# A hybrid S5 and retention layer on one core: an early read of kst in each S5 chunk, later S5 parameters and scaled q, and squares of x behind the next weight cast

## The chip, the cores and the metric

The kernel runs on one core of one Trainium2 chip. The metric is the device time in microseconds (us) of one execution of the whole program; less is better. Three runs of the kernel before gave 1424.38, 1423.64 and 1424.18, a median of 1424.18.

## The reference

One layer of a decoder for 256 prompt positions and 8 samples of 8 positions, 320 rows of x with 2048 columns in all, in float32. In short:

```
h = rms_norm(x, norm_mix)
u, q, k, v, g = split(h @ w_in)             # 1024 columns each
y = s5_mixer(u)                             # 64 groups of 16 channels, 64 complex states each
y = gelu(y + d*u); y = y * sigmoid(y @ w_glu + b_glu)
o = retention(rotary(q), rotary(k), v)      # 8 heads of 128, decay per head, chunks of 128
o = silu(g) * group_norm(o)
x = x + concat(y, o) @ w_out
x = x + (silu(gate) * up) @ w_ffn_out       # gate, up = split(rms_norm(x, norm_ffn) @ w_ffn_in)
return rms_norm(x, norm_final), the S5 states, the retention states
```

## The kernel before, in words

x lies transposed: 128 channels on the partitions, 320 rows as columns, 16 such pieces. Every weight matrix is cut in blocks of 128 columns by 8 pieces of 128 rows (512 KB). SyncE (SP) loads a block into raw, ScalarE (ACT) casts it to hi in a shorter float format (line 133), VectorE (DVE) takes lo = raw - hi (line 135). raw, hi and lo have three buffers each, so the load of a block waits for DVE's lo of the block three before it, and the cast to hi waits until TensorE (PE) has read the hi of three before. A product is three matmuls per piece: hi with xhi, hi with xlo, lo with xhi (lines 145 to 147), 24 matmuls for a block, all summed in PSUM.

**First stage** (lines 954 to 980). Four outputs (two blocks of u, q and k of head 0) are accumulated together while x arrives, piece by piece and then in pairs. For each pair ACT and DVE make xhi and xlo (split_x, lines 269 to 276), ACT casts the weights (line 967), DVE makes lo (line 968), and ACT squares x in place for the norm (square_x, line 280). Their place in ACT's queue comes from priorities. DVE's s5_params and s5_params2 work out powers of the S5 eigenvalues from then on; POOL makes exponentials for them.

**Projections and heads** (lines 1014 to 1035). PE's order is written out by hand: projections run one after the other, and a clock in the program (clk.now, advanced with each product) decides after which matmul a piece of other work is put in. For a head: rot turns q and k by the rotary angles on DVE (lines 725 to 733), do_q multiplies the sample part of q by a decay into qg (lines 893 to 896), head_k transposes k into pst, copies it to kd on ACT and makes the scores pss, head_v transposes v and makes the outputs po, the group norm and the new state.

**S5 chunks** (s5_chunk, from line 577). Eight chunks of eight groups. A chunk first writes u to DRAM (via) and reads it back in another layout into kst: eight DMAs on SP's queue (line 590), which kst's two buffers share between chunks. Some time later (DL["b1"]) PE transposes four blocks bl into pt (line 624), and ACT copies pt into bst. Later again (DL["b2"]) PE makes the outputs py of the chunk before (s5_outputs, which reads toe and kst of that chunk), and then pb from bst and kst (line 639). ACT copies a part of pb into toe, six DMAs on SP spread it in toe (line 654), and DVE scans over the positions. toe and pb have one buffer each.

SP issues all loads of weights, kst, toe and the rest in one queue, one after the other; its order, and those of ACT and DVE, come from a scheduler by priorities and dependencies. Two words of the language: issue_after(i) keeps instructions behind i in their engine's order, and high_priority lifts them in it.

Of the kernel before, what the change touches and what calls it, by code (L numbers as in the profile page):

```python
# [12 lines left out]
F32 = mybir.dt.float32  # L13
F32R = mybir.dt.float32r
I32 = mybir.dt.int32
AF = mybir.ActivationFunctionType
ALU = mybir.AluOpType
ADD, SUB, MUL = ALU.add, ALU.subtract, ALU.mult
PSUM = bass.MemoryType.PSUM

P = 128
D = 2048
KT = D // P
NP, NB, NS = 256, 8, 8
# [8 lines left out]
CH = 4  # L33
NCP = NP // CH
NC = N // CH
# [11 lines left out]
def hybrid_kernel(ctx, tc, xT, w_in, w_in4, w_out, w_glu, w_fi, w_fo, w_fot, gfr, vecs, s5p, bc, x0,  # L47
# [3 lines left out]
    pe, act, dve, pool, sp = nc.tensor, nc.scalar, nc.vector, nc.gpsimd, nc.sync  # L51

    cst = ctx.enter_context(tc.tile_pool(name="cst", bufs=1))
# [3 lines left out]
    def f(t):  # L57
        return t.bitcast(F32)


    ident = cst.tile([P, P], F32, name="ident")
    make_identity(nc, ident)
    ones = cst.tile([P, P], F32, name="ones")
    pool.memset(ones, 1.0)
    mhalf = cst.tile([P, 4], F32, name="mhalf")
    pool.memset(mhalf, -0.5)
    vec = cst.tile([P, vecs.shape[1]], F32, name="vec")
# [35 lines left out]
    def mm(cost, *a, **k):  # L103
        pe.matmul(*a, **k)
        clk.now += cost
# [73 lines left out]
    def tt(out, a, b, op):  # L179
        dve.tensor_tensor(out, a, b, op)  # L180
        return out
# [15 lines left out]
    EVAC = 1500  # L197
# [39 lines left out]
    ps_b = s5stack.enter_context(tc.tile_pool(name="ps_b", bufs=1, space=PSUM))  # L237
# [3 lines left out]
    def misc(name):  # L241
        used["misc"] = clk.now
        return ps_m.tile([P, 512], F32, name=name, tag="misc", bufs=2)
# [25 lines left out]
    def split_x(k0, k1):  # L269
        for k in range(k0, k1):  # L270
            xr = xrs[k // 4][:, k % 4]
            if k == 0:
                tt(xhi[:, k], xr, v("g_mix", k).to_broadcast([P, N]), MUL)
            else:
                act.mul(xhi[:, k], xr, v("g_mix", k))
            dve.scalar_tensor_tensor(xlo[:, k], xr, v("g_mix", k), f(xhi[:, k]), MUL, SUB)

    def square_x(k0, k1):
        xr = xrs[k0 // 4][:, k0 % 4:(k1 - 1) % 4 + 1]
        act.activation(xr, xr, AF.Square)  # L280
        if k1 == 8:
            tt(u32[:, 0:4], u32[:, 0:4], u32[:, 4:8], ADD)
        elif k1 == 12:
            tt(u32[:, 0:4], u32[:, 0:4], retp[:, 0:4], ADD)
        elif k1 > 12:
            a = u32[:, 0:2]
            tt(a, a, u32[:, 2:4] if k1 == 14 else retp[:, 6:8], ADD)
            if k1 == 14:
                tt(a, a, retp[:, 4:6], ADD)
            else:  # L290
                tt(a[:, 0], a[:, 0], a[:, 1], ADD)
        return u32[:, 0]
# [126 lines left out]
    def s5_params2(used):  # L419
        newscr(1)  # L420
        scr[1] = used
        tt(lp[:, 0, 0], rr, ec[:, 0], MUL)
        tt(lp[:, 1, 0], rr, es[:, 0], MUL)
        den = tt(T(sh), prm[:, 0], prm[:, 0], MUL)
        d2 = tt(T(sh), prm[:, 1], prm[:, 1], MUL)
        tt(den, den, d2, ADD)
        rden = T(sh)
        dve.reciprocal(rden, den)
        rot_t["rden"] = rden
# [147 lines left out]
    def s5_chunk(c):  # L577
# [42 lines left out]
            tbl = s5_table(c)  # L620
        bst = s5.tile([P, 4, P], F32, name="bst", tag="bst", bufs=1)
        pt = misc("pt")
        for i in range(4):
            tr(pt[:, P * i:P * i + P], bl[:, i // 2, i % 2].rearrange("p u e h -> p (u e h)"))
        with tc.high_priority(offset=EVAC):
# [3 lines left out]
        if c:  # L629
            while clk.now - used["misc"] < MISC:  # L630
                yield 0.4
            pending.pop()()
        pb = ps_b.tile([P, 2, 512], F32, name="pb", tag="pb", bufs=1)
        for i in range(4):
            for u in range(2):

# [20 lines left out]
        if c < 7:  # L657
            pending.append(lambda: s5_outputs(c, kst, cl, xp))
            return
        yield DL["scan"]  # L660
        while clk.now - used["misc"] < MISC:
            yield 0.4
        s5_outputs(c, kst, cl, xp)
# [54 lines left out]
    rot_t = {}  # L718

    def rot(ps, name):  # L720
        assert rot_t["ready"]
        with tc.high_priority(offset=EVAC):
            return rot_(ps, name)

    def rot_(ps, name):
        sw = mp.tile([P, N], F32, name="sw", tag="sw", bufs=1)
        act.copy(sw[0:64], ps[64:128])
        rot_t["keys"] = act.copy(sw[64:128], ps[0:64])
        a = mp.tile([P, N], F32, name=name, tag=name, bufs=1)
        tt(a, ps, csr[:, 0], MUL)  # L730
        tt(sw, sw, csr[:, 1], MUL)
        tt(a, a, sw, ADD)
        return a

    def head_k(h, q_, qg, k_, R):
# [25 lines left out]
    def head_v(h, v_, qg, rt, R):  # L761
# [5 lines left out]
        with tc.high_priority(offset=EVAC):  # L767
            for i in range(3):
                act.mul(vT[:, i], pst2[:, P * i:P * i + P], rtok[:, i:i + 1])
        act.copy(vsp[64 * (h % 2):64 * (h % 2) + 64], vT[64:128, 2])  # L770
        last = act.copy(vs[:, h], vT[64:128, 2])
        if h == 0:
            rot_t["values"] = last
# [24 lines left out]
        with tc.high_priority(offset=GN):  # L798
            for i in range(nt):
                dve.bn_stats(st[:, i], po[:, i])  # L800
                dve.bn_aggr(mv[:, :, i], st[:, i])

        m_, t_, y_, w_ = mv[:, 0], mv[:, 1], y[:, 0], y[:, 1]
        pool.tensor_scalar(m_, m_, -1.0, None, MUL)
# [6 lines left out]
        pool.tensor_tensor(w_, m_, y_, MUL)  # L811
        if h == 0:
            rot_t["first"]()
        on = mp.tile([P, 3, P], F32, name="on", tag="on", bufs=1)

        def normed():
# [59 lines left out]
    def do_q(h, ps=None):  # L876
        ps = proj(8 + 4 * h) if ps is None else ps
        R = HS[h]
        rt = mp.tile([P, NB, P], F32, name="rt", tag="rt", bufs=2)
        R["rt"] = rt  # L880
        for i in range(2 if h == 1 else min(h, 1)):
            i = i if h == 1 else h
            with tc.issue_after(last_raw[0].ins) if h == 1 else nullcontext():
                sp.dma_start(HS[i]["rt"], r0[i])
        mk = mp.tile([P, NP + P], F32, name="mk", tag="mk", bufs=2)
        n = NP + P if h % 2 else NP
        with nullcontext() if h else tc.issue_after(last_raw[0].ins):
            sp.dma_start(mk[:, 0:n], masks[h, :, 0:n])
        R["mk"] = mk
        q_ = rot(ps, "q_")  # L890
        pool.tensor_copy(qsp[:, 64 * (h % 2):64 * (h % 2) + 64], q_[:, NP:N])
        qg = qgs[h % 2]
        for u in range(2):
            tt(qg[:, u].rearrange("p (b w) -> p b w", w=40)[:, :, 0:NS],
               q_[:, NP + 32 * u:NP + 32 * u + 32].rearrange("p (b t) -> p b t", t=NS),
               gqt[:, h].unsqueeze(1).to_broadcast([P, 4, NS]), MUL)
        R.update(q_=q_, qg=qg)
        run_due()

    def do_k(h, ps=None):  # L900
        ps = proj(9 + 4 * h) if ps is None else ps
        R = HS[h]
        k_ = rot(ps, "k_")
        pool.tensor_tensor(kvf[:, h], k_[:, NP:N].rearrange("p (b t) -> p b t", t=NS),
                           kdt[:, h].unsqueeze(1).to_broadcast([P, NB, NS]), MUL)
        pool.tensor_copy(ksp[:, 64 * (h % 2):64 * (h % 2) + 64], k_[:, NP:N])
        spawn(head_k(h, R["q_"], R["qg"], k_, R))
        run_due()
# [45 lines left out]
    for k1 in (1, *range(2, KT + 1, 2)):  # L954
        with tc.high_priority(offset=100000), tc.manual_schedule(engines={mybir.EngineType.SP}):
            if k0 % 2 == 0:
                raw, hi, lo = (wp.tile([P, 8, P], d, name=n, tag=n, bufs=3).rearrange("p (k o) m -> p k o m", o=4)
                               for n, d in (("raw", F32), ("hi", F32R), ("lo", F32R)))
            q = slice(k0 % 2, (k1 - 1) % 2 + 1)
            sp.dma_start(xrs[k0 // 4][:, k0 % 4:(k1 - 1) % 4 + 1], xT[:, k0:k1])  # L960
            (sp if k0 else act).dma_start(raw[:, q], w_in4[:, k0:k1])
            if not k0:
                sp.dma_start(vec, vecs)
            if k1 == 4:
                sp.dma_start(prm, s5p)
            split_x(k0, k1)
            act.copy(hi[:, q], raw[:, q])
            los.append(dve.tensor_tensor(lo[:, q], raw[:, q], f(hi[:, q]), SUB))
        if k1 == 4:
            exps = s5_exps()  # L970
        if k1 % 2 == 0:
            with tc.high_priority(offset=50000):
                accq = square_x(k1 - 2, k1)
        for k in range(k0, k1):
            for w_, x_ in ((hi, xhi), (hi, xlo), (lo, xhi)):
                for i, ps in enumerate(accs):
                    pe.matmul(ps, w_[:, k % 2, i], x_[:, k], start=k == 0 and w_ is hi and x_ is xhi,
                              stop=k == KT - 1 and w_ is lo)
            clk.now += 1.6
        k0 = k1  # L980
# [8 lines left out]
    def finish_norm():  # L989
        next(rg)  # L990
        act.copy(rtok, ytok[0])
        yield 4.5
        rps = next(rg)
        with tc.high_priority(offset=EVAC):
            act.copy(rbc, rps)
            tt(csr[:, 0], csr[:, 0], rbc, MUL)
            turned = dve.tensor_tensor(csr[:, 1], csr[:, 1], rbc, MUL)
            tt(u32[:, 0], ps0, rbc, MUL)
            tt(u32[:, 1], ps1, rbc, MUL)
        rot_t["ready"] = True  # L1000

        with tc.issue_after(turned.ins):
            s5_params2(exps[1])

    spawn(finish_norm(), DL["nm"])

# [538 lines left out]
```

## Time and profile before

| what | value |
|---|---|
| median of three runs | 1424.18 us |
| the profiled execution | 1424.95 us |
| its span | 1423.2 us |
| PE busy | 1415.5 us, 99% |
| DVE, ACT, POOL busy | 957.9, 606.5, 122.8 us |
| DMA, mean over the span | 188 GB/s |

The profile is one execution taken by the hardware profiler. PE is TensorE, DVE VectorE, ACT ScalarE, POOL GpSimd, SPq SyncE's queue of DMA issues. A row of a timeline gives start, duration, engine, line, operation, output<-inputs, shape, count, and in brackets the idle time of the engine before it with what ended it. A row of the list of waits gives who waited for whom, then us in total, times, longest us. A row of a table by stretches gives the stretch, its length, the busy time (and instructions) of PE, PE's weight loads, DVE, ACT and POOL, then the granted clock of PE as a share of full speed, the DMA share and GB/s. Names such as kst stand for every buffer of that name.

### The profile page before, as it was taken

The numbers are of one execution on the slowest core, as the hardware profiler recorded it, in microseconds if no ns is written. First come the engines' busy times: TensorE is split into PE (matmuls) and PEld (weight loads), VectorE is DVE, ScalarE is ACT, GpSimd is POOL, SyncE is SP. The second block draws the span as 40 slices with busy tenths as digits, with TensorE's granted clock in tenths as the row PEclk, the third lists the DMA queues.
The fourth block names the chain that finished last, engine by engine and source line by source line (L and its number), as shares of the span: only waits on it lengthen the run. The fifth ranks groups of instructions, "written<-read, shape, count | busy, mean of one in ns | idle before, by whom it ended". The sixth has DMA issues, their size and how long they took to land.

```text
span 1423.2 us, 26196 instructions
## 1 busy us (share of the span) xinstructions
PE 1415.5 (99%) x10376; PEld 1406.6 (99%) x10376; DVE 957.9 (67%) x1842; ACT 606.5 (43%) x973; POOL 122.8 (9%) x194
## 2 busy tenths in 40 slices
PE   9999999999999999999999999999999999999998
PEld 8999999999999999999999999999999999999998
DVE  7979878787557747777777545767644677655453
ACT  6654555555455443333333333333333333334553
POOL 7720111110000000100001000000000000000002
PEclk9999999999999999999999999999999999999999
DMA  8554555555644466675666446666545765445542
GB/s 278 170 187 158 163 174 157 171 163 157 218 156 151 164 209 228 221 253 201 245 206 231 136 148 238 233 216 235 170 146 175 255 233 190 159 157 184 154 143 75
DMA packets 102316, 267.07 MB, mean 188 GB/s; under 512 B 27377, under 2 KB 42033, under 8 KB 102193
## 3 DMA queue, kind: packets, MB, share of 16 engines
q1 hardware_dynamic: 101904, 265.01, 55.9%
q8 instruction: 81, 1.33, 0.4%
q10 hardware_dynamic: 288, 0.39, 0.1%
q14 instruction: 43, 0.34, 0.1%
HBM read 254.44 MB, written 10.52 MB: 186 GB/s over the span
## 4 chain that ended last, share of the span: by engine, by line
PE 96%; DVE 2%; DMA 1%; ACT 1%; issue 1%; POOL 0%; SPq 0%; POOLq 0%; DVEq 0%; ACTq 0%
PE ps_fg L147 7%; PE ps_fu L147 7%; PE ps_fu L146 7%; PE ps_fg L146 7%; PE ps_fg L145 7%; PE ps_fu L145 7%; PE ps_fo L147 7%; PE ps_fo L145 7%; PE ps_fo L146 7%; PE ps_p L145 6%; PE ps_p L147 6%; PE ps_p L146 6%; PE ps_o L145 2%; PE ps_o L146 2%; PE ps_o L147 2%; PE ps_t L1342 1%
## 5 line engine op out<-in xcount | busy, mean ns | idle before, releaser
L133 ACT CAST hi<-raw 128x1024 fp32r<-128x1024 f32 (+1 forms) x410 | 397.8, 971 | 684.2 <-PE ps_fg L146 182.3
L135 DVE TENSOR_TENSOR lo<-raw,hi 128x1024 fp32r<-128x1024 f32 (+1 forms) x410 | 462.8, 1129 | 304.2 <-ACT hi L133 301.3
L147 PE MATMUL ps_fg<-hhi,lo 128*128 128x320 f32 x704 | 218.0, 310 | 0.0
L147 PE MATMUL ps_fu<-hhi,lo 128*128 128x320 f32 x704 | 217.9, 310 | 0.0
L145 PE MATMUL ps_fg<-hhi,hi 128*128 128x320 f32 x704 | 217.9, 310 | 0.0
L146 PE MATMUL ps_fu<-hlo,hi 128*128 128x320 f32 x704 | 217.9, 310 | 0.0
L145 PE MATMUL ps_fu<-hhi,hi 128*128 128x320 f32 x704 | 217.9, 310 | 0.0
L146 PE MATMUL ps_fg<-hlo,hi 128*128 128x320 f32 x704 | 217.9, 310 | 0.0
L145 PE MATMUL ps_fo<-ahl,hi 128*128 128x320 f32 x671 | 208.0, 310 | 0.0
L147 PE MATMUL ps_fo<-ahl,lo 128*128 128x320 f32 x671 | 207.7, 310 | 0.0
L146 PE MATMUL ps_fo<-ahl,hi 128*128 128x320 f32 x671 | 207.7, 310 | 0.0
L145 PE MATMUL ps_p<-xhi,hi 128*128 128x320 f32 x560 | 177.3, 317 | 0.0
L147 PE MATMUL ps_p<-xhi,lo 128*128 128x320 f32 x560 | 173.3, 309 | 0.0
L146 PE MATMUL ps_p<-xlo,hi 128*128 128x320 f32 x560 | 173.1, 309 | 0.0
L147 PEld LDWEIGHTS ps_fg<-hhi,lo 128*128 128x128 f32 x704 | 132.2, 188 | 0.0
L146 PEld LDWEIGHTS ps_fu<-hlo,hi 128*128 128x128 f32 x704 | 132.2, 188 | 0.0
L146 PEld LDWEIGHTS ps_fg<-hlo,hi 128*128 128x128 f32 x704 | 132.2, 188 | 0.0
L145 PEld LDWEIGHTS ps_fg<-hhi,hi 128*128 128x128 f32 x704 | 132.2, 188 | 0.0
L147 PEld LDWEIGHTS ps_fu<-hhi,lo 128*128 128x128 f32 x704 | 132.1, 188 | 0.0
L145 PEld LDWEIGHTS ps_fu<-hhi,hi 128*128 128x128 f32 x704 | 132.1, 188 | 0.0
L146 PEld LDWEIGHTS ps_fo<-ahl,hi 128*128 128x128 f32 x671 | 126.0, 188 | 0.0
L147 PEld LDWEIGHTS ps_fo<-ahl,lo 128*128 128x128 f32 x671 | 126.0, 188 | 0.0
(476 smaller groups left out, 2117.8 us busy)
## 6 DMA issues: line engine op xcount, KB each, us to landing
raw<-w_fi SPq DMA_DIRECT2D x176, 512.0 KB, 4.2
raw<-w_in SPq DMA_DIRECT2D x79, 512.0 KB, 4.1
raw<-w_fo SPq DMA_DIRECT2D x61, 512.0 KB, 3.5
raw<-w_out SPq DMA_DIRECT2D x32, 512.0 KB, 3.7
hi<-vd SPq DMA_DIRECT2D x32, 512.0 KB, 5.4
lo<-vd SPq DMA_DIRECT2D x32, 512.0 KB, 5.2
raw<-w_fo SPq DMA_DIRECT2D x61, 192.0 KB, 2.4
rt<-r SPq DMA_DIRECT2D x8, 512.0 KB, 5.2
```

Source lines behind the costliest of these rows:

```text
L133: cast = act.copy(hi[:, :m], raw[:, :m])
L135: last_lo[0] = dve.tensor_tensor(lo[:, :m], raw[:, :m], f(hi[:, :m]), SUB)
L145: pe.matmul(ps, hi, xhi[:, k], start=k == 0, stop=False)
L146: pe.matmul(ps, hi, xlo[:, k], start=False, stop=False)
L147: pe.matmul(ps, lo, xhi[:, k], start=False, stop=k == nk - 1)
L1342: pe.matmul(ps[0:m, 0:TC], a3[:, x_, k, s:s + m], w_[:, k], start=k == 0 and x_ == 0 and w_ is whi, stop=k == FCT - 1 and w_ is wlo)
```

## The change

- **Early read of kst.** In s5_chunk, for chunks 1 to 7, pb is allocated ahead of the transposes, and a matmul of 3 columns by 1 reads toe and kst of the chunk and writes three unused values of pb, ahead of the transposes pt. Its result is not used.
- **First stage.** The squares of pairs (0,1) and (2,3) and those after them are issued behind the next pair's cast, the split of x and the cast behind an earlier square; the cast of the second pair is split in two halves, and so is its lo. ones is set by DVE, not POOL.
- **Head 0.** s5_params2 is issued behind the rotation of k and no longer behind the scaling of csr. The scaled q of head 0 (qg) is issued behind head 0's group statistics.
- **Small.** The copy to vsp gets a higher priority for odd heads; the last chunk's outputs wait 1.2 longer on the program's clock.

```diff
@@ s5_chunk
         pt = misc("pt")
+        pb = ps_b.tile([P, 2, 512], F32, name="pb", tag="pb", bufs=1)
+        if c:
+            mm(0.06, pb[0:CH - 1, 1, 4 * NC:4 * NC + 1], toe[:, 0, 0:CH - 1, 0], kst[:, 0, 0:1], start=True, stop=True)
         for i in range(4):
...
-        pb = ps_b.tile([P, 2, 512], F32, name="pb", tag="pb", bufs=1)
...
-        yield DL["scan"]
+        yield DL["scan"] + 1.2
@@ head_v
-        act.copy(vsp[64 * (h % 2):64 * (h % 2) + 64], vT[64:128, 2])
+        with tc.high_priority(offset=EVAC if h % 2 else 0):
+            act.copy(vsp[64 * (h % 2):64 * (h % 2) + 64], vT[64:128, 2])
...
         if h == 0:
             rot_t["first"]()
+            with tc.issue_after(aggr.ins):
+                R["scaled_q"]()
@@ do_k
         k_ = rot(ps, "k_")
+        if not h:
+            with tc.issue_after(rot_t["turned"].ins):
+                s5_params2(exps[1])
@@ the first stage
-            split_x(k0, k1)
-            act.copy(hi[:, q], raw[:, q])
-            los.append(dve.tensor_tensor(lo[:, q], raw[:, q], f(hi[:, q]), SUB))
+            with tc.issue_after(sq[-1].ins) if len(sq) > 1 and k1 < 10 else nullcontext():
+                split_x(k0, k1)
+                for q in ([slice(i, i + 1) for i in range(2)] if k1 == 4 else [q]):
+                    cast = act.copy(hi[:, q], raw[:, q])
+                    los.append(dve.tensor_tensor(lo[:, q], raw[:, q], f(hi[:, q]), SUB))
...
-        if k1 % 2 == 0:
-            with tc.high_priority(offset=50000):
-                accq = square_x(k1 - 2, k1)
+        for k2 in {1: (), 2: (), 4: (2,), 6: (4,), 8: (6, 8)}.get(k1, (k1,)):
+            with tc.high_priority(offset=50000), tc.issue_after(cast.ins):
+                accq = square_x(k2 - 2, k2)
```

What stands in the engines' orders, before and now. First ACT's queue at the start of the first stage: hi is the weight cast, xhi the scaled x, u<-u the square. Before:

```order
L967 CAST hi<-raw 128x512
L275 ACTIVATE xhi<-u_119,vec 128x320
L967 CAST hi<-raw 128x512
L280 ACTIVATE u_119<-u_119 128x640
L275 ACTIVATE xhi<-u_119,vec 128x320 x2
L967 CAST hi<-raw 128x1024
L280 ACTIVATE u_119<-u_119 128x640
```

Now:

```order
L984 CAST hi<-raw 128x512
L275 ACTIVATE xhi<-u_119,vec 128x320
L984 CAST hi<-raw 128x512
L275 ACTIVATE xhi<-u_119,vec 128x320 x2
L984 CAST hi<-raw 128x512 x2
L282 ACTIVATE u_119<-u_119 128x640
```

The first square has moved behind the second pair's cast, and this cast is two.

Next PE's queue at chunk 2, inside a projection (ps_p); bl is what is transposed into pt. Before:

```order
L145 MATMUL ps_p_2065<-xhi_101,hi_2054 128x320
L146 MATMUL ps_p_2065<-xlo_102,hi_2054 128x320
L147 MATMUL ps_p_2065<-xhi_101,lo_2055 128x320
L109 MATMUL pt_2079<-ident_64,bl_1888 128x128 x4
L145 MATMUL ps_p_2065<-xhi_101,hi_2054 128x320
```

Now:

```order
L145 MATMUL ps_p_2068<-xhi_101,hi_2057 128x320
L146 MATMUL ps_p_2068<-xlo_102,hi_2057 128x320
L147 MATMUL ps_p_2068<-xhi_101,lo_2058 128x320
L104 MATMUL pb_2083<-kst_1873,toe_144 3x1
L109 MATMUL pt_2082<-ident_64,bl_1891 128x128 x4
L145 MATMUL ps_p_2068<-xhi_101,hi_2057 128x320
```

The new matmul stands at the place of the transposes, and reads chunk 2's kst, kst_1873. In chunks 1 to 5 it does so between the same matmuls as the transposes before; in chunks 6 and 7 both stand three projection matmuls earlier.

Last SP's queue for the same chunk, now, with the semaphores that SP waits for: the last six of the eight pieces of kst_1873, and the weight loads (raw) between them.

```order
L592 DMA kst_1873<-via_1871 16x4x80 [waits DMAHW7_49]
L592 DMA kst_1873<-via_1871 16x4x80 [waits DMAHW0_49]
L592 DMA kst_1873<-via_1871 16x4x80 [waits DMAHW1_49]
L132 DMA raw_2314<-w_in 128x1024 [waits DMAHW2_49,DVE_49]
L592 DMA kst_1873<-via_1871 16x4x80 [waits DMAHW3_49]
L592 DMA kst_1873<-via_1871 16x4x80 [waits DMAHW4_49]
L132 DMA raw_2320<-w_in 128x1024 [waits DMAHW5_49,DVE_49]
L592 DMA kst_1873<-via_1871 16x4x80 [waits DMAHW6_49]
```

Here nothing has moved: the queue before reads the same with line 590 in place of 592. In chunks 5 and 6 one piece of kst is left behind the last such weight load, where there were two and three.

On DVE at head 0 the scaled q stood between the rotations of q and k, with lp and scrt of s5_params2 around it; now lp, scrt and the reciprocal follow the rotation of k, and the scaled q follows the group statistics.

More of the change, by code (lines that the diff above doesn't have):

```diff
@@ L61, in hybrid_kernel @@
     ident = cst.tile([P, P], F32, name="ident")
+    ones = cst.tile([P, P], F32, name="ones")
+    dve.memset(ones, 1.0)
     make_identity(nc, ident)
-    ones = cst.tile([P, P], F32, name="ones")
-    pool.memset(ones, 1.0)
     mhalf = cst.tile([P, 4], F32, name="mhalf")
@@ L276, in split_x @@
             dve.scalar_tensor_tensor(xlo[:, k], xr, v("g_mix", k), f(xhi[:, k]), MUL, SUB)
+    sq = []
     def square_x(k0, k1):
         xr = xrs[k0 // 4][:, k0 % 4:(k1 - 1) % 4 + 1]
-        act.activation(xr, xr, AF.Square)
+        sq.append(act.activation(xr, xr, AF.Square))
         if k1 == 8:
@@ L731, in rot_ @@
         tt(sw, sw, csr[:, 1], MUL)
-        tt(a, a, sw, ADD)
+        rot_t["turned"] = dve.tensor_tensor(a, a, sw, ADD)
         return a
@@ L800, in head_v @@
                 dve.bn_stats(st[:, i], po[:, i])
-                dve.bn_aggr(mv[:, :, i], st[:, i])
+                aggr = dve.bn_aggr(mv[:, :, i], st[:, i])
         m_, t_, y_, w_ = mv[:, 0], mv[:, 1], y[:, 0], y[:, 1]
@@ L892, in do_q, with scaled_q @@
         qg = qgs[h % 2]
[L893 to L897, printed above, removed]
+        def scaled_q():
+            for u in range(2):
+                tt(qg[:, u].rearrange("p (b w) -> p b w", w=40)[:, :, 0:NS],
+                   q_[:, NP + 32 * u:NP + 32 * u + 32].rearrange("p (b t) -> p b t", t=NS),
+                   gqt[:, h].unsqueeze(1).to_broadcast([P, 4, NS]), MUL)
+        R.update(q_=q_, qg=qg, scaled_q=scaled_q)
+        if h:
+            scaled_q()
         run_due()
@@ L996, in finish_norm @@
             tt(csr[:, 0], csr[:, 0], rbc, MUL)
-            turned = dve.tensor_tensor(csr[:, 1], csr[:, 1], rbc, MUL)
+            tt(csr[:, 1], csr[:, 1], rbc, MUL)
             tt(u32[:, 0], ps0, rbc, MUL)
@@ L1000, in finish_norm @@
         rot_t["ready"] = True
-        with tc.issue_after(turned.ins):
-            s5_params2(exps[1])
     spawn(finish_norm(), DL["nm"])
```

## The prediction

> **What bounds the kernel now.** I read the page's busy shares first, then what PE waited for, then the timelines of the places that the change touches.
>
> ```profile
> span 1423.2 us, 26196 instructions
> ...
> PE 1415.5 (99%) x10376; PEld 1406.6 (99%) x10376; DVE 957.9 (67%) x1842; ACT 606.5 (43%) x973; POOL 122.8 (9%) x194
> ```
>
> PE is busy for all but 7.7 us of the span. So only two things move the end: PE time that disappears from those 7.7 us, and new time in which PE stands still. PE's list of waits is short (us in total, times, longest):
>
> ```profile
> PE warm_ps L118 <- POOL ones L64: 1.1, 1, 1.1
> PE py L977 <- ACT hi L967: 0.9, 2, 0.6
> PE py L977 <- DVE xhi L180: 0.5, 1, 0.5
> PE pst L109 <- DVE k__737 L180: 0.3, 1, 0.3
> PE pst L109 <- ACT kd L743: 0.3, 1, 0.3
> PE py L977 <- DVE xlo L276: 0.2, 1, 0.2
> ```
>
> These 3.3 us all lie before 56 us; the rest of the idle time is at the very end, which the diff leaves alone. Nowhere in the S5 chunks does PE wait: at present nothing is there to be won. The change aims at the second, fourth and fifth row.
>
> **The first stage.** ACT casts the weights of one pair in one go, after the squares of x and the two scaled copies of x:
>
> ```profile
> 7.14 0.62 ACT L967 CAST hi<-raw 128x512 fp32r<-128x512 f32 x1 [1.80 <-DMA raw<-w_in]
> 7.67 0.73 ACT L280 ACTIVATE u<-u 128x640 f32<-128x640 f32 x1
> 8.31 1.00 ACT L275 ACTIVATE xhi<-u,vec 128x320 fp32r<-128x320 f32 x2
> 9.31 1.05 ACT L967 CAST hi<-raw 128x1024 fp32r<-128x1024 f32 x1
> ```
>
> The double cast ends at 10.36 and PE's longest wait of 0.6 us ends with it. Split, its first half takes 0.62 as in the first of these rows: if the weights landed only just before 9.31, PE starts 1.05 - 0.62 = 0.43 us sooner. With the square (0.64 us to the next start) out of the way it could start earlier still, if the weights are there, but no more than the 0.6 us of the wait can go. I take 0.43, with 0 and 0.6 as ends (no loss: what is moved behind the cast, the square, is needed only by the sum of squares at the end of the stage). The other squares that move delay casts of later pairs by at most one square, 0.64; PE's list has no wait for a cast after the second, so ACT is ahead of PE there. The memset of ones on DVE costs nothing: DVE's first other instruction waits for vec anyway, and PE's row "DVE xhi" holds whatever the warm-up wins or loses, up to 0.5.
>
> **The first head.** Between the rotations of q and k, DVE carries pieces of the S5 parameters and the scaled q:
>
> ```profile
> 47.18 0.82 DVE L180 TENSOR_TENSOR lp<-rr,ecs 128x32 f32<-128x32 f32 x2
> 48.32 1.11 DVE L180 TENSOR_TENSOR scrt<-prm 128x32 f32<-128x32 f32 x2
> 49.36 0.79 DVE L180 TENSOR_TENSOR qg<-q__727,gqt 128x32 f32<-128x32 f32 x2
> 52.71 0.34 DVE L428 RECIPROCAL scrt<-scrt 128x32 f32<-128x32 f32 x1
> 52.98 0.67 DVE L180 TENSOR_TENSOR k__737<-k__737,sw 128x320 f32<-128x320 f32 x1
> ```
>
> Put behind the last row, they bring k forward by 0.82 + 1.11 + 0.79 + 0.34 = 3.1 us, less what the ends of neighbours overlap. PE waited 0.3 for k and would come 0.43 earlier, so 0.7 would do; the wait goes. The gate's silu on ACT also comes earlier and no longer stands ahead of the kd copies, so the second 0.3 goes too. Worth 0.6, between 0 and 0.6. The moved pieces then stand ahead of the score masks, for which DVE has time until PE's next product, and the scaled q is read only by head 1. The exchange of vsp and vs, and the 1.2 added to the last chunk's delay, change no place in PE's order that matters (the last chunk's outputs stand after the same projection step): 0, either way at most the 0.3 of a small copy.
>
> **The early wait.** This is where the time is decided. In chunks 1 to 7 a matmul of 3x1 now stands ahead of the four transposes pt, and it reads kst (filled by eight DMAs) and toe. PE takes its instructions in order, so behind it wait the transposes, and the projection matmuls that follow. Before, kst was read first by pb, some 8 us later. Here is when PE comes to pt in chunks 1 to 7:
>
> ```profile
> 111.44 0.60 PE L109 MATMUL pt<-ident,bl 128*128 128x128 f32 x4
> 144.68 0.60 PE L109 MATMUL pt<-ident,bl 128*128 128x128 f32 x4
> 180.67 0.60 PE L109 MATMUL pt<-ident,bl 128*128 128x128 f32 x4
> 216.01 0.60 PE L109 MATMUL pt<-ident,bl 128*128 128x128 f32 x4
> 251.09 0.60 PE L109 MATMUL pt<-ident,bl 128*128 128x128 f32 x4
> 286.55 0.60 PE L109 MATMUL pt<-ident,bl 128*128 128x128 f32 x4
> 322.07 0.60 PE L109 MATMUL pt<-ident,bl 128*128 128x128 f32 x4
> ```
>
> And here is when SP issues the last pieces of kst in the same seven chunks (start, time of issue); for chunk 2 with the weight load ahead of it:
>
> ```profile
> 94.09 1.06 SPq L590 DMA_DIRECT2D kst<-via  x2
> ...
> 148.65 0.35 SPq L132 DMA_DIRECT2D raw<-w_in  x1
> 149.04 0.43 SPq L590 DMA_DIRECT2D kst<-via  x1
> ...
> 178.66 0.90 SPq L590 DMA_DIRECT2D kst<-via  x2
> ...
> 217.82 0.43 SPq L590 DMA_DIRECT2D kst<-via  x1
> ...
> 252.17 1.34 SPq L590 DMA_DIRECT2D kst<-via  x2
> ...
> 287.49 1.37 SPq L590 DMA_DIRECT2D kst<-via  x3
> ...
> 317.32 1.84 SPq L590 DMA_DIRECT2D kst<-via  x4
> ```
>
> The time from issue to landing of all 64 of them, and SP's largest wait between 100 and 160 us:
>
> ```profile
> DMA to landing us min/median/max: 1.6/3.4/4.5
> ```
>
> ```profile
> SPq L132 <- DVE lo L135: 31.4, 11, 6.7
> ```
>
> In chunk 2 the last piece lands at about 149.04 + 3.4 = 152.44, and PE stands at the new matmul from 144.68: 7.8 us. It cannot come earlier, since in SP's queue it stands behind a weight load that waits for DVE's lo of an earlier block. With 3.4 in each chunk: chunk 1 has landed long before (0); chunk 3 (second of two, 179.11 + 3.4 - 180.67) 1.8; chunk 4 (217.82 + 3.4 - 216.01) 5.2; chunk 5, where the new order leaves one piece behind the weight load, (252.17 + 3.4 - 251.09) 4.5; chunk 6, also one, and PE comes three projection matmuls earlier (1415.5 us for 10376 instructions is 0.14 each, so 0.4), (287.49 + 3.4 - 286.15) 4.7; chunk 7 (318.70 + 3.4 - 321.67) 0.4. The sum is 24.4. A shift of everything by the 1.0 won earlier leaves the differences as they are, since the loads follow blocks that PE has finished. With the shortest landing, 1.6, each is 1.8 less and the sum 15; with the longest, 4.5, it is 31. None of it comes back: before, the pb row that follows in chunk 2 found its data there, as PE's list shows, so no wait is saved.
>
> ```profile
> 153.35 0.41 PE L104 MATMUL pb<-kst,bst 64*64 64x80 f32 x8
> ```
>
> The matmul's own cost: the nearest are six of one column, 0.72 us together, 0.12 each; seven make 0.8 (0 to 1.5).
>
> ```profile
> 36.12 0.72 PE L104 MATMUL ps_r<-ones,u 128*128 128x1 f32 x6
> ```
>
> **PE after a wait.** PE is slower for a time after it has stood still. Eight warm-up matmuls took 0.434 us each at the start; ten of the same took 0.247 each near the end. And the granted clock fell when the work was over:
>
> ```profile
> 1.12 3.47 PE L118 MATMUL warm_ps<-ones 128*128 128x512 f32 x8 [1.12 <-POOL ones L64]
> ...
> 1415.66 2.47 PE L118 MATMUL warm_ps<-ones 128*128 128x512 f32 x10
> 1418.17 0.63 PE L1366 MATMUL ps_b<-ident,ahl 64*128 64x64 f32 x4
> ```
>
> ```profile
> 1420.00:1421.00 1.00, 0.00 (x0) 0.00 (x0) 0.00 (x0) 0.00 (x0) 0.00 (x0) 0.82 0.93 266
> ```
>
> A mean of 0.82 over that microsecond, with half speed as the lower state, puts the fall at 1420.64, 1.84 us after the last matmul's end at 1418.80. The waits of chunks 2, 4, 5 and 6 are well longer. One restart costs about 8 x (0.434 - 0.247) = 1.5 us, four cost 6.0. Chunk 3's 1.8 is on the edge; I count none for it.
>
> The Trainium skill (TensorE: Matmul & The Clock Gate, section "What's actually happening") says that the clock halves after at least one idle window of about 3.4 us, and that the windows run freely. By that rule a wait of 4.5 to 5.2 us holds a whole window only in 3 to 5 cases of 10, so two drops or three, not four, and an estimate from that page is about 1452. The row above has the clock fall sooner than that, so I keep four.
>
> **The sum.** The profiled execution took 1424.95, 0.77 above the median of 1424.18. 1424.95 - 0.43 - 0.6 + 0.8 + 24.4 + 6.0 = 1455.1, which at the median is 1454.4.
>
> **The rivals.**
> 1. The waits come, but the clock stays up in all but perhaps the longest. For: the 0.6 us waits of the first stage left it up, and nothing in the trace lies between those and 1.84. Time: 1454.4 - 6.0 = 1448.4.
> 2. The waits do not come, so that the change does not do what its order says: the last pieces of kst land before PE reaches the new matmul. That decides when they are issued 3.4 us ahead of pt, in chunk 2 at 141.3 and not 149.0. Against it: the weight load in front, released by DVE. Time: 1424.18 - 1.03 + 0.8 = 1423.95, no slower than before.
> 3. The waits come with landings near 1.6, because the queue is empty while PE stands: 24.4 falls to 15, and with the clock's 6.0 the time is 1445; if the clock stays up too, 1439.
> 4. The waits are longer: landings of 4.5 (31), a fifth restart, and ACT held up too, since the copy of pt into bst now waits at the head of ACT's queue with weight casts behind it: 1424.18 - 0.23 + 31 + 7.5 = 1462.5 or more.
>
> **How the numbers follow.** Forecast 0.60, rival 1 0.20, rival 2 0.05, rival 3 0.08, rival 4 0.07. The predicted time is 1454.4. From 1444 to 1461 lie the forecast with its bounds, rival 1 and the upper half of rival 3; rivals 2 and 4 and the rest are left out, some 0.16. About 0.2% (2.8 us) is what a measurement of this kernel can tell from no change; every case but rival 2 lies above it, so slower 0.94, same 0.05, faster 0.01.
>
> **What would show it.** Right: PE's list of waits gains rows of the matmul into pb, released by DMA kst, some five of them, the longest near 8 us in chunk 2, 24 us together; PE's idle time grows by as much; the granted clock shows halves after them; the rows on ACT hi, k and kd shrink or go. Wrong: no such rows, or PE busy for all but 7 us as before; then the pieces of kst must be issued earlier against pt than in the rows above. If the waits are there and the granted clock stays at 1.00 to the end, rival 1 holds.

## The result

The changed kernel takes 1461.92 us (median of 5, 1461.26 to 1462.96), the kernel before 1424.07 (5 runs beside it): 1.0267 times as long, interval 1.0252 to 1.0282. The forecast was 1454.4, its range ended at 1461.0. The profiled execution took 1462.96, the highest of the five. From its page, the span and the busy times:

```profile
span 1461.2 us, 26200 instructions
...
PE 1426.6 (98%) x10390; PEld 1415.7 (97%) x10390; DVE 960.1 (66%) x1844; ACT 607.5 (42%) x974; POOL 127.6 (9%) x193
```

PE stands still for 34.6 us where it was 7.7, and is busy for 1426.6 us where it was 1415.5. So the 38.0 us by which the span has grown have two parts: 26.9 of standing still, 11.1 of longer work. PE's list of waits, from its head (us in total, times, longest):

```profile
PE pb L104 <- DMA via<-up__2357: 8.2, 1, 8.2
PE pb L104 <- DMA kst<-via: 7.3, 2, 4.9
PE pb L104 <- DMA mk<-masks: 6.0, 1, 6.0
PE pb L104 <- DMA via<-up__4367: 5.5, 1, 5.5
...
PE ps_p L147 <- DVE lo L135: 0.7, 2, 0.5
```

The four first rows are new. All are the 3x1 matmul into pb. The transfers named are those that landed at that moment; three of the names are of no tile that the matmul reads, so what it waited for has to be found out (below). The same matmul in the timeline of PE, chunks 2 to 7, with the wait ahead of it in brackets (in chunk 1 it waits for nothing):

```profile
153.49 0.19 PE L104 MATMUL pb<-kst,toe 128*3 128x1 f32 x2 [8.16 <-DMA via<-up__2357]
194.26 0.19 PE L104 MATMUL pb<-kst,toe 128*3 128x1 f32 x2 [2.35 <-DMA kst<-via]
235.75 0.19 PE L104 MATMUL pb<-kst,toe 128*3 128x1 f32 x2 [5.95 <-DMA mk<-masks]
278.29 0.19 PE L104 MATMUL pb<-kst,toe 128*3 128x1 f32 x2 [4.91 <-DMA kst<-via]
320.68 0.19 PE L104 MATMUL pb<-kst,toe 128*3 128x1 f32 x2 [5.50 <-DMA via<-up__4367]
359.37 0.19 PE L104 MATMUL pb<-kst,toe 128*3 128x1 f32 x2 [0.43 <-DMA rp_o<-rp]
```

That is 27.3 us in six waits; forecast were 24.4 in the same six chunks. SP's queue for the longest of them, chunk 2:

```profile
149.10 0.35 SPq L132 DMA_DIRECT2D raw<-w_in  x1
149.50 0.43 SPq L592 DMA_DIRECT2D kst<-via  x1
```

The last piece of kst is issued at 149.50, behind the weight load, and the matmul starts 3.99 us later, where the forecast, from the rows of the kernel before, had 149.04 and 3.4 us. SP had to wait for DVE's lo before it could issue that weight load; its longest wait for lo between 140 and 150 us is 5.3 us.

The longer work is the clock's for the most part. While PE has work left, the granted clock falls to a half four times, from 148.97, 234.30, 278.67 and 319.63 on, for 10.24, 6.83, 3.41 and 6.83 us: one, two or three times 3.41 us. Cut into stretches of that length from the first fall, chunks 2, 3 and 5 look like this (stretch, length, busy time of PE, PEld, DVE, ACT and POOL with instructions, granted clock, DMA share, GB/s):

```profile
145.55:148.97 3.42, 0.00 (x0) 0.00 (x0) 2.51 (x4) 1.71 (x3) 0.00 (x0) 1.00 0.00 1
148.97:152.38 3.41, 0.00 (x0) 0.00 (x0) 0.10 (x1) 0.00 (x0) 0.00 (x0) 0.50 0.62 198
152.38:155.79 3.41, 2.30 (x11) 2.30 (x12) 0.00 (x0) 0.59 (x1) 0.00 (x0) 0.50 0.34 111
155.79:159.21 3.42, 3.42 (x14) 3.42 (x14) 0.44 (x1) 1.04 (x1) 0.00 (x0) 0.50 0.00 0
...
189.93:193.34 3.41, 1.98 (x29) 1.51 (x18) 1.48 (x8) 0.86 (x3) 1.09 (x3) 1.00 0.62 204
193.34:196.75 3.41, 2.49 (x19) 2.49 (x20) 0.00 (x0) 1.74 (x5) 1.23 (x6) 1.00 0.81 255
...
271.85:275.26 3.41, 1.53 (x12) 1.27 (x10) 1.83 (x3) 2.46 (x7) 0.00 (x0) 1.00 0.34 95
275.26:278.67 3.41, 0.38 (x4) 0.38 (x5) 0.00 (x0) 0.00 (x0) 0.00 (x0) 1.00 0.78 267
278.67:282.09 3.42, 3.42 (x16) 3.42 (x15) 0.81 (x2) 1.64 (x2) 0.00 (x0) 0.50 0.03 7
```

The first column behind the length is PE, the figure behind the five engines the clock. Each stretch has one clock, and the next stretch's follows from how much PE worked in this one: after a stretch of 0.00 or 0.38 it is a half, after one of 2.30 at half speed it stays there, after one of 3.42 it is full again. What half speed costs, by the projection matmuls of PE's timeline on both sides of 159.21:

```profile
156.12 0.47 PE L145 MATMUL ps_p<-xhi,hi 128*128 128x320 f32 x1
156.39 0.47 PE L146 MATMUL ps_p<-xlo,hi 128*128 128x320 f32 x1
...
159.42 0.31 PE L146 MATMUL ps_p<-xlo,hi 128*128 128x320 f32 x1
159.57 0.30 PE L147 MATMUL ps_p<-xhi,lo 128*128 128x320 f32 x1
```

From start to start they are 0.267 us apart, then 0.147: of each microsecond worked at half speed 0.45 is lost. PE works 2.30 + 3.42 us at half speed in chunk 2, 3.42 in chunk 5, and 5.4 and 5.8 in chunks 4 and 6; together 20.3, and 9.1 us lost. Of the 11.1 of longer work that leaves 2.0 for something else (run 3).

### The profile page after: what moved, and what is told of

It is laid out like the page before. It is cut to its first block, busy times and chain, and to the rows that moved or that the text cites. A ratio compares the mean times of both kernels' runs of the same rounds, so it can differ in the third digit from the quotient of the medians.

```text
span 1461.2 us, 26200 instructions
## 1 busy us (share of the span) xinstructions
PE 1426.6 (98%) x10390; PEld 1415.7 (97%) x10390; DVE 960.1 (66%) x1844; ACT 607.5 (42%) x974; POOL 127.6 (9%) x193
## 4 chain that ended last, share of the span: by engine, by line
PE 84%; DVE 8%; DMA 3%; issue 2%; ACT 1%; SPq 1%; POOL 1%; POOLq 0%; DVEq 0%
PE ps_fu L146 7%; PE ps_fg L146 7%; PE ps_fg L147 7%; PE ps_fg L145 7%; PE ps_fu L147 7%; PE ps_fu L145 7%; PE ps_fo L145 7%; PE ps_fo L146 7%; PE ps_fo L147 7%; DVE lo L135 3%; PE ps_o L145 2%; PE ps_o L147 2%; PE ps_o L146 2%; PE ps_p L145 2%; PE ps_p L146 2%; PE ps_p L147 2%
## 5 line engine op out<-in xcount | busy, mean ns | idle before, releaser
L145 PE MATMUL ps_p<-xhi,hi 128*128 128x320 f32 x560 | 180.4, 322 | 0.0
```

What stands on the lines that cost most here:

```text
L145: pe.matmul(ps, hi, xhi[:, k], start=k == 0, stop=False)
```

## The experiments

Theory A: the read of kst ahead of the transposes makes the whole loss, by waits for the last pieces in SP's queue and by the clock that falls behind them; the rest of the change is worth about -1. Rivals: the early allocation of pb and the moved instructions make a part; another operand is what is waited for; the longer work is not the clock's.

**1. The changed kernel without the early read.**

```diff
-            mm(0.06, pb[0:CH - 1, 1, 4 * NC:4 * NC + 1], toe[:, 0, 0:CH - 1, 0], kst[:, 0, 0:1], start=True, stop=True)
+            clk.now += 0.06
```

> The changed kernel without its 3x1 matmul (pb is still allocated early, the program's clock still counts its 0.06). Theory A, the read of kst ahead of the transposes makes the whole loss: the matmul's 27 us of waits, the some 10 us of slow clock behind them and its own 0.8 all go, and what is left is the first stage and head 0, so 1423.0 to 1423.7 against 1424.1 for the kernel before; PE idle for 6.5 to 7.5 us, no row of pb in PE's waits. Theory B, the early allocation of pb and the other moved instructions make a part of it: some of the waits stay and the time is 1430 or more.

Measured: 1424.32 us (11 runs, 1423.66 to 1425.06) against 1424.01; ratio 1.0000, 0.9991 to 1.0008. All of the loss is gone. PE's waits, the whole list:

```profile
PE warm_ps L118 <- DVE ones L63: 1.0, 1, 1.0
PE ps_p L147 <- DVE lo L135: 0.5, 1, 0.5
PE py L994 <- DVE xhi L180: 0.4, 1, 0.4
```

The waits for hi, k and kd that the change aimed at are gone, and one for lo is new. The time is above the 1423.0 to 1423.7 expected: by the two profiled spans (1422.2 and 1423.2) the rest of the change is worth -1.0, by the medians +0.3, and the interval holds both. The profiled execution of the kernel before was on the long side (1424.95), so its span flatters the change. No gain is shown.

**2. The early read alone, on the kernel before.**

```diff
         pt = misc("pt")
+        pb = ps_b.tile([P, 2, 512], F32, name="pb", tag="pb", bufs=1)
+        if c:
+            mm(0.06, pb[0:CH - 1, 1, 4 * NC:4 * NC + 1], toe[:, 0, 0:CH - 1, 0], kst[:, 0, 0:1], start=True, stop=True)
...
-        pb = ps_b.tile([P, 2, 512], F32, name="pb", tag="pb", bufs=1)
...
-        yield DL["scan"]
+        yield DL["scan"] + 1.2
```

> The kernel before with the early pb, the 3x1 matmul and the last chunk's 1.2 alone. Theory A: the whole loss and without the small gain, so 1462 to 1463.5; the same waits in chunks 2 to 7, 26 to 28 us together. Theory B: the loss needs the first stage's or head 0's new order too, so well under 1455.

Measured: 1461.77 (1461.21 to 1463.17), ratio 1.0263, 1.0249 to 1.0277; 27.0 us of waits. With run 1 this leaves nothing of the loss to the other parts. Its clock falls five times, not four: in chunk 3 too, whose wait is shorter here (2.00, against 2.35 in the changed kernel, where the clock stayed up). The stretches there:

```profile
190.10:193.51 3.41, 1.41 (x12) 1.19 (x11) 0.00 (x0) 0.38 (x2) 2.32 (x8) 1.00 0.73 178
193.51:196.93 3.42, 3.42 (x15) 3.42 (x14) 1.02 (x1) 2.29 (x5) 0.00 (x0) 0.50 0.94 367
```

The whole wait of 2.00 lies in one stretch and leaves PE 1.41 us of work in it. In the changed kernel the wait of 2.35 was cut by the border at 193.34, and left 1.98 and 2.49 of work. So it is not the length of a wait that decides.

**3. The early read without kst.** Its result is unused either way.

```diff
-            mm(0.06, pb[0:CH - 1, 1, 4 * NC:4 * NC + 1], toe[:, 0, 0:CH - 1, 0], kst[:, 0, 0:1], start=True, stop=True)
+            mm(0.06, pb[0:CH - 1, 1, 4 * NC:4 * NC + 1], toe[:, 0, 0:CH - 1, 0], ident[:, 0:1], start=True, stop=True)
```

> The changed kernel with the 3x1 matmul at its new place, reading toe and a column of the identity in place of kst (its result is unused either way). Theory A, the last pieces of kst are what is waited for: no waits, no falls of the clock, 1423.5 to 1424.5. Rival: toe, or the place in pb, is what is waited for, and the trace's name of the DMA is off: 1462 as before the edit. If the matmul itself costs far more than 0.12 us each, 1425 to 1427.

Measured: 1426.36 (10 runs, 1425.80 to 1427.23), ratio 1.0014, 1.0005 to 1.0023. No row of pb in PE's waits, the clock up to the end: kst was waited for. But 2.0 us are left against run 1. Chunk 1 in PE's timeline, first without the matmul (run 1), then with it:

```profile
110.30 0.31 PE L147 MATMUL ps_p<-xhi,lo 128*128 128x320 f32 x1
...
110.81 0.39 PE L145 MATMUL ps_p<-xhi,hi 128*128 128x320 f32 x1
```

```profile
110.56 0.31 PE L147 MATMUL ps_p<-xhi,lo 128*128 128x320 f32 x1
110.80 0.19 PE L104 MATMUL pb<-ident,toe 128*3 128x1 f32 x2
...
111.33 0.39 PE L145 MATMUL ps_p<-xhi,hi 128*128 128x320 f32 x1
```

The rows left out are the four transposes. From one projection matmul to the next it is 0.51 us without and 0.77 with, and 0.50 and 0.78 in chunk 2: the matmul costs 0.26 at this place, seven of them 1.8.

**4. The waits filled with work.** The added matmuls' result is overwritten.

```diff
+        for _ in range((0, 0, 28, 4, 20, 16, 18, 0)[c]):
+            pe.matmul(pb[:, 1], onesr, onesr.unsqueeze(1).to_broadcast([P, 4, P]), start=True, stop=True)
         if c:
             mm(0.06, pb[0:CH - 1, 1, 4 * NC:4 * NC + 1], toe[:, 0, 0:CH - 1, 0], kst[:, 0, 0:1], start=True, stop=True)
```

> The changed kernel with 28, 4, 20, 16 and 18 matmuls of 512 columns ahead of the 3x1 matmul of chunks 2 to 6 (some 0.22 us each at full clock; their result is overwritten), so that PE works through most of each wait and stands still for about 1 to 3 us at a time. Theory A1, the time over the waits themselves is the clock's: the waits and fillers together still take 27 us, the granted clock stays up, and the some 10 us go, so about 1452. Theory A2, the extra busy time comes from something else (slower reads behind the waits, later operands): 1460 to 1463 with the clock up. If the fillers overshoot the landings, 1454 to 1456 with hardly a wait left.

Measured: 1455.15 (1453.58 to 1455.30), the clock at full until the work is over. PE does 86 matmuls of 512 columns more than the changed kernel, and is done 6.8 us sooner. The 3x1 matmul's group, with its idle time as the first figure behind the second bar, in this kernel:

```profile
L104 PE MATMUL pb<-kst,toe 128*3 128x1 f32 x14 | 1.3, 164 | 9.2 <-DMA kst<-via 4.5 <-DMA via<-up__2385 1.8 <-DMA raw<-w_in 1.8
```

The waits left are of 1.1 to 1.8 us, and none brought the clock down. By the pages, against run 3 (span 1424.2, PE busy 1417.4): here PE works 19.4 longer and stands still 9.9 longer, 29.3; in the changed kernel 9.2 and 27.8. So the time that the reads hold PE up is the same but for 1.5, most of it a wait of 1.7 in chunk 7 in place of 0.43, and the 9.2 of longer work is the clock's. That bears out A1; the 1452 expected lacked those 1.5 and took 10 for the clock, and the last microsecond is within the spread of the runs.

**5. kst's transfers put ahead.**

```diff
-        for i in range(2):
-            for e in range(CH):
-                sp.dma_start(kst[64 * i + 16 * e:64 * i + 16 * e + 16],
...
+        with tc.high_priority(offset=1500):
+            for i in range(2):
+                for e in range(CH):
+                    sp.dma_start(kst[64 * i + 16 * e:64 * i + 16 * e + 16],
...
```

> The changed kernel with the eight kst transfers of each chunk put ahead of later weight loads in SP's queue, so that the last of them is issued some 20 us sooner; PE's order is as in the changed kernel. Theory A, what is waited for are the last pieces of kst behind a weight load that waits for DVE: no waits at the 3x1 matmul, the clock stays up, and what is left is the matmul's own 0.26 each as in the run that reads toe alone: 1425.8 to 1427. Rival: the waits only move, since the weight loads now stand behind kst's pieces and PE waits for lo or hi instead: 1430 or more, with rows of ps_p in PE's waits.

Measured: 1457.00 (1456.70 to 1457.36), ratio 1.0232. The expectation failed: all waits but 5 us are still there, at the same matmul. PE's list, and SP's queue ahead of the matmul of chunk 2 (which starts at 150.46 after a wait of 5.50):

```profile
PE pb L104 <- DMA toe<-toe: 11.3, 4, 4.7
PE pb L104 <- DMA raw_bc<-bc: 5.5, 1, 5.5
PE pb L104 <- DMA mk<-masks: 5.3, 1, 5.3
```

```profile
146.10 0.35 SPq L132 DMA_DIRECT2D raw<-w_in  x1
146.50 1.24 SPq L659 DMA_DIRECT2D toe<-toe  x2
```

kst's pieces went to 120 to 128 us, and toe's, which the matmul reads too, went back: the last two now stand behind the weight load, where the last piece of kst had stood. In the changed kernel the last of them was issued at 138.42.

**6. Is it toe?** The same with the read of toe taken out.

```diff
-            mm(0.06, pb[0:CH - 1, 1, 4 * NC:4 * NC + 1], toe[:, 0, 0:CH - 1, 0], kst[:, 0, 0:1], start=True, stop=True)
+            mm(0.06, pb[0:CH - 1, 1, 4 * NC:4 * NC + 1], ident[:, 0:CH - 1], kst[:, 0, 0:1], start=True, stop=True)
```

> The changed kernel with kst's transfers put ahead, as in the run that took 1457.0, and the 3x1 matmul reading kst and a column of the identity, not toe. Theory A: the waits left in that run were for toe, whose last pieces had come to stand behind a weight load; without the read of toe none is left, 1425.8 to 1427. Rival: those waits were for kst after all: 1455 to 1458 again.

Measured: 1425.91 (10 runs, 1425.54 to 1426.22), no waits of pb, no fall. It was toe. With runs 3 and 5: the matmul waits for whichever of its tiles has its last pieces behind a weight load that DVE has not yet released.

**7. kst's and toe's transfers both put ahead** (toe's with the same offset of 1500).

```diff
-        with tc.high_priority(offset=4 * EVAC if c == 7 else 0):
+        with tc.high_priority(offset=1500):
             for u in range(2):
                 for t in range(CH - 1):
...
```

> The changed kernel with kst's and toe's transfers both put ahead of later weight loads, so that two to four weight loads stand behind the last of them when PE comes. Theory A, the 3x1 matmul waits for whichever of its two tiles has pieces behind a weight load that waits for DVE: no waits now, the clock stays up, 1425.8 to 1427, the time of the run that reads toe with its transfers where they were. Rival, whatever stands last in the queue takes the place (the weight loads come late, and PE waits for lo): 1430 or more with rows of ps_p.

Measured: 1432.44 (1430.90 to 1433.21), ratio 1.0056. No waits at the 3x1 matmul any more, but two new ones elsewhere, 1.0 us for POOL's ksp and this one:

```profile
PE py L104 <- ACT retp L862: 3.4, 1, 3.4
```

The first brings the clock down once. Theory A holds for the matmul, and the rival for what comes next, though by other engines than it named. Where retp's delay begins can be read in the same trace, from SP's queue, DVE and ACT:

```profile
329.62 0.35 SPq L132 DMA_DIRECT2D raw<-w_out  x1
330.01 0.90 SPq L704 DMA_DIRECT2D yc<-back  x2
...
334.93 0.76 DVE L184 SCALAR_TENSOR_TENSOR y<-u,vec,yc 128x320 f32<-128x320 f32 x1 [3.17 <-DMA yc<-back]
...
335.73 0.47 ACT L712 ACTIVATE y<-y 128x320 f32<-128x320 f32 x1 [4.29 <-DVE y L184]
...
336.70 0.86 ACT L862 ACTIVATE retp<-pn,vec 128x256 f32<-128x256 f32 x3
```

yc is the tile into which SP reads back the S5 outputs. Its last two pieces now stand behind a weight load; DVE's y waits for them, ACT's next step on y waits for DVE, and retp stands behind that step in ACT's queue. In run 1 retp starts at 328.08. So a third tile has come into the place behind a weight load; this is read from the trace, and no run takes the read of yc away. Why ksp comes late was not followed up.

**8. The early read moved behind the outputs, right ahead of pb.**

```diff
-        if c:
-            mm(0.06, pb[0:CH - 1, 1, 4 * NC:4 * NC + 1], toe[:, 0, 0:CH - 1, 0], kst[:, 0, 0:1], start=True, stop=True)
...
             pending.pop()()
+            mm(0.06, pb[0:CH - 1, 1, 4 * NC:4 * NC + 1], toe[:, 0, 0:CH - 1, 0], kst[:, 0, 0:1], start=True, stop=True)
```

> The changed kernel with the 3x1 matmul moved some 8 us later, right ahead of the matmuls into pb that read all of kst. Theory A, the place alone makes the waits: none here, 1425 to 1427 with the matmul's own cost of 0.26 each at most. Rival, the read as such is slow wherever it stands (a first touch of kst after its transfers): some waits stay, 1430 or more.

Measured: 1425.14 (10 runs, 1424.62 to 1426.23). The group's idle time is nothing:

```profile
L104 PE MATMUL pb<-kst,toe 128*3 128x1 f32 x14 | 1.4, 166 | 0.0
```

The same read of the same tiles, some 9 us later, waits for nothing. The time is 0.8 above run 1, 0.12 for each of the seven matmuls, so at this place they cost less than half of what they do ahead of the transposes. The place alone makes the waits.

**9. and 10. One chunk alone.** The same line for 2 and for 3:

```diff
-        if c:
+        if c and c != 2:
+            clk.now += 0.06
+        if c == 2:
             mm(0.06, pb[0:CH - 1, 1, 4 * NC:4 * NC + 1], toe[:, 0, 0:CH - 1, 0], kst[:, 0, 0:1], start=True, stop=True)
```

> The changed kernel with the 3x1 matmul in chunk 2 alone. Theory A, each chunk's wait stands by itself: 1424.3 without any of them, and 8.2 for the wait, 0.26 for the matmul and 1.6 to 2.9 for working at half the clock behind it, so 1434.4 to 1435.7. Rival, the waits depend on each other (what PE loses in one chunk the transfers gain in the next): the wait in chunk 2 alone comes out other than 8.2, or the loss shows elsewhere too.

> The changed kernel with the 3x1 matmul in chunk 3 alone, whose wait was 2.35 us without a fall of the clock in one kernel and 2.00 us with one in the other. Theory C, the clock is set at the end of windows of 3.41 us that run on by themselves, by how much PE stood still within one, and some 1.9 to 2.0 us decide: a wait of 2.0 to 2.4 us gives a fall in the executions where it lies inside one window, so the times spread from 1426.5 (no fall) to 1428.8 (a fall, 1.7 of work lost), and the profiled execution shows the fall or not as the wait lies. Rival, only a window in which PE stands still all the time lowers the clock: never a fall, all times at 1426.3 to 1427.3.

Chunk 2: 1434.45 (1433.68 to 1435.05), 10.1 above run 1, with a wait of 8.2 as among the others. So the wait of chunk 2 stands by itself, and what PE loses in it is not won back later. Chunk 3: 1428.09 (8 runs, 1426.88 to 1428.67): two runs at 1426.9, six from 1427.75 up, as without and with a fall. In the profiled one (1428.36) the wait was 2.63 (2.35 where chunk 2 had waited too), and the stretches around it:

```profile
180.28:183.70 3.42, 1.19 (x10) 1.18 (x11) 0.00 (x0) 0.57 (x2) 2.27 (x8) 1.00 0.82 224
183.70:187.11 3.41, 3.41 (x15) 3.41 (x14) 1.01 (x1) 2.11 (x4) 0.00 (x0) 0.50 0.78 305
```

PE did not stand still for the whole of the first stretch, and yet the clock fell at its end. Theory C holds against its rival in the trace; for the other runs the two groups only fit it, since one execution of a kernel is profiled.

**11. The first stage alone, on the kernel before**: ones by DVE, the split cast and the moved squares, as in the diff of the change.

```diff
-            split_x(k0, k1)
-            act.copy(hi[:, q], raw[:, q])
...
+            with tc.issue_after(sq[-1].ins) if len(sq) > 1 and k1 < 10 else nullcontext():
+                split_x(k0, k1)
+                for q in ([slice(i, i + 1) for i in range(2)] if k1 == 4 else [q]):
+                    cast = act.copy(hi[:, q], raw[:, q])
...
-        if k1 % 2 == 0:
-            with tc.high_priority(offset=50000):
+        for k2 in {1: (), 2: (), 4: (2,), 6: (4,), 8: (6, 8)}.get(k1, (k1,)):
+            with tc.high_priority(offset=50000), tc.issue_after(cast.ins):
```

> The kernel before with the first stage's part of the change alone: the squares behind the next cast, the second pair's cast split, ones set by DVE. The profile of the changed kernel had the second pair begin 0.25 us sooner, and a wait of 0.5 for a lo that came back behind it. Theory: worth 0 to 0.5 us, so a median of 1423.5 to 1424.1 against 1424.0, not to be told from no change by the time, but to be seen in the trace: PE's wait for hi shrinks from 0.6 to 0.4 or less, and a wait of ps_p for DVE lo is new. Rival: the first stage is what gave back the second 0.6 of head 0 too, by a slower lo; then the time is above 1424.5.

Measured: 1424.69 (11 runs, 1424.31 to 1425.26) against 1424.18; ratio 1.0003, 0.9995 to 1.0012. PE's waits for hi are gone altogether, and these two, later in the program, are new:

```profile
PE ps_p L147 <- DVE lo L135: 0.6, 1, 0.6
PE po L104 <- ACT vsp L772: 0.5, 1, 0.5
```

It looks as if PE gave back, where it comes too early for a later operand, what it gains in the first stage, but no run shows it by the time: the run with the old first stage (run 2) has no such row for lo, the runs with the new one have 0.4 to 0.9. The median came out above the range expected, on the rival's side, but the interval holds no change.

## Why the prediction was nearly right, and where it failed

The direction, the place, the six chunks and the mechanism were right: PE at the head of its order waits for the last pieces of kst, which SP can't issue before DVE releases the weight load in front. Rivals 2 and 3 fell (the waits came, at full length), and rival 1 too (the clock fell). The time came out 7.5 above the forecast, beyond the range by 0.9. The step that failed is the sizing of the sum: three of its terms were too small, and the gain that it took off is not shown.

- **Landing.** 24.4 rested on the median of 3.4 us from issue to landing. That is the median of all the pieces; in the changed kernel the matmul starts 3.4 to 4.3 us after the issue of the last one (3.99 in chunk 2). The waits were 27.3: 2.9 more.
- **The clock.** This is the largest miss. One restart was put at 1.5, and four were counted. Four is what the profile has, and 1.5 is what one stretch of 3.41 us at half speed costs (3.41 x 0.45). But in three of the four waits PE came back within a stretch that was already lost, worked the rest of it at half speed, and then the whole of the next. 20.3 us of such work cost 9.1 and not 6.0. Chunk 3, called on the edge, was: no fall here, a fall in run 2.
- **The matmul.** 0.12 each, from six matmuls of one column that stood together; 0.26 here, where one stands by itself between projections and transposes. 1.8 and not 0.8, which is what the seven cost in run 8.
- **The first stage and head 0.** -1.03 was counted to the end. The waits did go in run 1, but a wait for lo came in their place (0.5 there, 0.7 in the changed kernel): the step asked what is late next only of the moved pieces, not of the weights' lo. By medians nothing is left of the gain, but the interval (-1.3 to +1.1 in run 1) holds the forecast too, so that this term was wrong is not shown.

Between the two profiled executions the span grew by 38.0 where the forecast's terms make 30.2. Of the 7.8 missed, landing, clock and matmul are 2.9 + 3.1 + 1.0 = 7.0. PE's standing still elsewhere fell by 0.4 (from 7.7 to 34.6 - 27.3) where 1.03 was forecast, which is 0.6 more, and 0.2 of longer work stays unexplained. Rival 4's 1462.5 is close to the measured time, but mostly for other reasons: its landings of 4.5 and its fifth restart were not there. ACT was held up as it said (its copies into bst waited 23.7 us for PE), but PE's list has no new wait for a weight cast of ACT.

The prediction set a row against a page: the Trainium skill (TensorE: Matmul & The Clock Gate, section "What's actually happening") has windows of some 3.4 us that run freely, and a fall after an idle one. The trace agrees with the windows: every fall and rise lies on multiples of 3.41 us. It doesn't agree that the window has to be idle: runs 2 and 10 had falls after windows with 1.41 and 1.19 us of work. The prediction's own reading, that 1.84 us of standing still bring the clock down, was wrong as a rule: 2.35 us in chunk 3 did not. The fall that it was read from is a border too: the stretch of the kernel before that ends at 1420.63 holds 1.54 us of work. Four was right for another reason than the one given: with a limit of some 1.5 us of work in 3.41 (last section), a wait of 4.9 us or more has at least half of its length, some 2.45 us, in one stretch and leaves less than 1.0 us of work there, wherever it falls. That chunk 3 had no fall in this execution was luck.

## What to carry to other kernels

An instruction placed early in an in-order engine's queue takes everything behind it to the landing of its last operand; ask of every tile that it reads where its last transfer stands in its queue, and what the transfer in front of that one waits for. Moving one transfer ahead moves another back (runs 5 and 7), so look at the whole queue and not at the one tile. When PE must stand still, count the clock beside the wait: here a quarter of the loss was work at half speed after the waits, not the waits.

## What the runs showed of the hardware that was not expected

In these traces the clock is decided stretch by stretch of 3.41 us, by how much PE works in it, and the limit is narrow. At full clock, PE was busy for 1.53 us in a stretch of the changed kernel that was followed by full speed (271.85, above), and for 1.47 in one of run 5 that was followed by half; in the latter the stretch ahead, of 1.56, was not:

```profile
268.05:271.47 3.42, 1.56 (x12) 1.30 (x10) 1.57 (x2) 2.20 (x6) 0.00 (x0) 1.00 0.72 222
271.47:274.88 3.41, 1.47 (x12) 1.47 (x13) 0.98 (x2) 2.01 (x5) 0.00 (x0) 1.00 0.59 163
274.88:278.29 3.41, 3.41 (x16) 3.24 (x14) 1.72 (x2) 1.04 (x1) 0.00 (x0) 0.50 0.05 11
```

So in these runs some 1.5 us of work in 3.41 held the clock up. The limit is not exact: the stretch at the end of the kernel before fell with 1.54, of which 0.6 were small 64x64 matmuls. At half speed more was needed to get it back: 2.30 us of work in a stretch was not enough (152.38 in the changed kernel), 3.06 was (run 7, after its wait for retp):

```profile
337.27:340.68 3.41, 3.06 (x80) 2.90 (x82) 2.73 (x7) 2.54 (x7) 0.00 (x0) 0.50 0.41 154
340.68:344.10 3.42, 3.42 (x36) 3.38 (x35) 2.89 (x12) 0.82 (x5) 0.00 (x0) 1.00 0.72 209
```

This need not be a second limit. A matmul takes 0.267 us at half speed and 0.147 at full, so counted in work these stretches hold 1.3 and 1.7 us at full speed, and one limit near 1.5 fits them as well; no run tells the two readings apart.

A wait of about 2 us therefore costs 0 or some 1.5 us more, by where it falls against the stretches, and by the two groups of run 10 that differs from one execution of the same kernel to the next.
